# Two weight chunks in a row at one matmul length: regrouped matmuls and four moved or merged steps in a two-block decoder

## The chip, the cores and the metric

One NeuronCore of one Trainium2 chip runs the whole program in one launch. The metric is the device time of an execution in microseconds (us). Two runs are told apart here from about 0.2%, that is 2.5 us.

## The reference

256 tokens of width 1024 pass through two decoder blocks in float32. Cut to what matters:

```
x = x + 0.5*swiglu(rmsnorm(x))                      # ff1, 1024 -> 2816 -> 1024
p = rmsnorm(x) @ w_in                               # gates g_a g_b, u, v, q, k, v of the branches
y_a = u * (W_s @ layernorm(v) + b)                  # spatial gating, branch a
y_b = stick_breaking_attention(q, k, v)             # branch b
x = x + (g_a*(y_a @ w_branch_a) + g_b*(y_b @ w_branch_b)) @ w_out
x = rmsnorm(x + 0.5*swiglu(rmsnorm(x)))             # ff2
h = x + moba(rmsnorm(x)) @ w_o;  h = h + relu(rmsnorm(h) @ w_up)^2 @ w_down      # mlp1
k, v, log_f = (rmsnorm(h)*g_kv) @ (w_kv, w_f)       # log_f: forget gate of 16 heads
h = h + fox(rmsnorm(h) @ w_q, k, v, cumsum(log_f)) @ w_o
h = h + relu(rmsnorm(h) @ w_up)^2 @ w_down                                       # mlp2
return rmsnorm(h)
```

## The kernel before

Nearly all work is weight times activation in float32, done as three products of rounded parts: a weight is split into a high and a low part, an activation too, and high·high, high·low and low·high are summed in PSUM. Weights stream from memory in chunks of 128x1024. For each chunk ScalarE copies the high part (`split_hi`, L140, tile `whi`, 5 buffers), VectorE subtracts it from the raw chunk to get the low part (`split_lo`, L147, tile `wlo`, 4 buffers) and TensorE multiplies (`unit_mm`, L150 to L239, its matmuls at L158).

In a **wide** group the activation's high and low parts lie side by side, so that `whi` takes one matmul of 512 columns where `wlo` takes one of 256. A wide group of the ff1, ff2, gate, gu and mlp stages has 4 chunks of 8 + 8 matmuls and 4 PSUM banks; groups take the banks of two rings (psA, psB) in turn. A down projection (`down`, L593) has 2 groups of 11 or 16 chunks. `orders` sets which kind comes first: high then low in a chunk, low then high in the next.

A unit is one chunk of one group (or a few chunks at the end of a group, `stagger`). The main loop goes over the units and issues, for unit u: the steps registered with `pre`, the high part of chunk u+3 and the low part of chunk u+2, the steps registered with `mid`, the matmuls, and the steps registered with `at`. This fixes the order on every engine; an engine runs its list in that order, and VectorE shares its list between `wlo` subtractions and all evacuations, norms and gating. A `wlo` subtraction needs the `wlo` buffer of four chunks before, so TensorE must be done with that chunk's low matmuls.

A norm (`norm_at`, L407) sums squares on VectorE, reduces them with two matmuls (L440), takes a square root on ScalarE (L443) and a reciprocal on VectorE (L448), while the first group of the stage multiplies the raw activation; the scale is applied to the outputs. The step `f` (L473 to L480) turns the scale into a column with two transposes (L477) and a copy (`rcol`, L479).

Other places that the change touches: `all_gains` (L1333) transposes the norm weights once into `gcol` (L1335 to L1337); `brB` (L906) is the second branch's projection, whose first PSUM banks wait for the gating of the first branch (L920); `fox_f0` to `fox_f4` (L1094 to L1157) compute the forget gate with 24 matmuls (L1104 to L1106) and a scan.

Of the kernel before, what the change touches and what calls it, by code (L numbers as in the profile page):

```python
# [26 lines left out]
class Group:  # L27
# [2 lines left out]

    def __init__(self, ring, srcs, ktiles, xin, tok=False, stagger=0, wide=False):
        self.ring, self.srcs, self.ktiles, self.xin = ring, srcs, ktiles, xin
        self.tok, self.stagger, self.wide = tok, stagger, wide
        self.width = sum(c for _, _, c in srcs)
        self.banks = self.width // (128 if wide else 256)
        self.kph = 1024 // self.width
        self.ps = None
# [3 lines left out]
def decoder_kernel(  # L43
# [58 lines left out]
    def add(g):  # L102
        g.u0 = len(units)
        hs = []
        for k0 in range(0, g.ktiles, g.kph):
            hs.append(len(halves))
            halves.append((g, k0))
        n = len(hs) - g.stagger
        units.extend((g, [h]) for h in hs[:n])
        if g.stagger:  # L110
            units.append((g, hs[n:]))
        g.u1 = len(units) - 1
        return g
# [36 lines left out]
    def unit_mm(u):  # L150
        g, hs = units[u]
        if g.ps is None:
            g.ps = [bank(g.ring) for _ in range(g.banks)]
            g.started = [False] * g.banks
        seq = [(h, kl) for h in hs for kl in range(g.kph)]

        def mm(b, dst, lhsT, rhs, stop):
            PE.matmul(dst, lhsT, rhs, start=not g.started[b], stop=stop, skip_group_check=True)  # L158
            g.started[b] = True

        def orders(i):

            return (("hi", "lo") if i % 2 == 0 or u < 4 else ("lo", "hi")) if g.wide else ((0, 1, 2),)

        def ws(h, kl, b, parts=(0, 1, 2), end=True):
            k = halves[h][1] + kl
            last = end and k == g.ktiles - 1
            if g.wide:
                col = kl * g.width + b * 128
                wh, wl = hi_t[h][:, col:col + 128], lo_t[h][:, col:col + 128]  # L170
                x = g.xin(k, b)
                if parts == "hi":
                    mm(b, g.ps[b], wh, both(x), last)
                elif parts == "lo":
                    mm(b, g.ps[b][:, :T], wl, x[:, 0, :], last)
                for i in parts if len(parts) == 1 else ():
                    mm(b, g.ps[b][:, T:] if i == 1 else g.ps[b][:, :T], wl if i == 2 else wh,
                       x[:, int(i == 1), :], False)
                return
            for j in range(2):  # L180
                nt = 2 * b + j
                col = kl * g.width + nt * 128
                wh, wl = hi_t[h][:, col:col + 128], lo_t[h][:, col:col + 128]
                x = g.xin(k, nt)
                dst = g.ps[b][:, j * T:(j + 1) * T]
                for i in parts:
                    mm(b, dst, wl if i == 2 else wh, x[:, int(i == 1), :], last and j == 1 and i == 2)

        def tsm(h, kl, tok, chs, c=slice(0, 512), d=0):
            k = halves[h][1] + kl  # L190
            last = k == g.ktiles - 1
            nch = g.width // 512
            xh, xl = (g.xin(k, 0)[:, i, tok * 128:(tok + 1) * 128] for i in range(2))
            for w in (hi_t[h], lo_t[h]):
                for ch in chs:
                    col = kl * g.width + ch * 512
                    b = tok * nch + ch + d
                    mm(b, g.ps[b][:, :c.stop - c.start], xh, w[:, col + c.start:col + c.stop], False)
            for ch in chs:
                col = kl * g.width + ch * 512  # L200
                b = tok * nch + ch + d
                mm(b, g.ps[b][:, :c.stop - c.start], xl, hi_t[h][:, col + c.start:col + c.stop], last)

        if g.tok:
            nch = g.width // 512
            if len(hs) > 1:
                for b in range(g.banks):
                    n = 1 if b < g.banks - 1 else 2
                    for i in range(n):
                        if i:  # L210
                            g.ps.append(bank(flip(g.ring)))
                            g.started.append(False)
                        for h, kl in seq:
                            tsm(h, kl, b // nch, (b % nch,), slice(i * 512 // n, (i + 1) * 512 // n), i)
            else:
                for h, kl in seq:
                    for tok in range(2):
                        tsm(h, kl, tok, range(nch))
        elif len(hs) > 1:
            for b in range(g.banks):  # L220
                o = orders(u - g.u0 + b)
                for i in o:
                    for h, kl in seq:
                        ws(h, kl, b, i, i == o[-1])
        elif u == 0:
            for b in range(g.banks):
                if b == 2:
                    x_bank(1)
                for i in range(3):
                    for h, kl in seq:  # L230
                        ws(h, kl, b, (i,))
        else:
            o = orders(u - g.u0)
            for i in o:
                if u == 1 and i == o[-1]:
                    x_turn(3)
                for h, kl in seq:
                    for b in range(g.banks):
                        ws(h, kl, b, i, i == o[-1])  # L239
# [167 lines left out]
    def norm_at(u, ring, two=False, cols=False, own=False):  # L407
# [93 lines left out]
        else:  # L501
            pre(v + 1, d)
        if cols:
            at(u0 + 7, f)

    def colsof(base, i=0):
        return gcol[:, base + 8 * i:base + 8 * i + 8]
# [33 lines left out]
    def ffn(ring, name, wg, wu, wd, slots):  # L541
        r, lead = ring, None
        for i in range(DFF // 256):
            g = add(Group(r, [(wg, 256 * i, 256), (wu, 256 * i, 256)], 8, hn_in, wide=True))
            if lead is None:
                lead = g
                at(g.u0, hidden(name, slots))
                norm_at(g.u0, r, own=True)
# [43 lines left out]

    def down(r, w, ktiles, xin, stagger=2):  # L593

        return [add(Group((r, flip(r))[i], [(w, 512 * i, 512)], ktiles, xin, stagger=i * stagger, wide=True))
                for i in range(2)]

    at(10, w_s_prep, B)
    for i in range(3):
# [33 lines left out]
    gates = []  # L633
    for i in range(4):
        gates.append(add(Group(r, [(win, 5120 + i * 512, 512)], 8, hn_in, wide=True)))
        r = flip(r)
    norm_at(gates[0].u0, gates[0].ring, cols=True, own=True)
    lnp = {}
# [37 lines left out]
    for i in range(2):  # L676
        r = flip(r)
        gu.append(add(Group(r, [(win, 512 * i, 512)], 8, hn_in, wide=True)))

    def gv_evac(b):  # L680
        if b == 0:
# [215 lines left out]
    def last_pv(u, name):  # L897
# [5 lines left out]
    at(qs[0].u1, hidden("yb", (1, 2)))  # L903
    brA = [add(Group(QR, [(w_branch_a[0], 512 * i, 512)], 8, lambda k, nt: xpair(cur["ya"], k)))
           for i in range(2)]
    brB = add(Group(QR, [(w_branch_b[0], 0, D)], 8, fixed_in("yb"), stagger=2))  # L906
    pus = pair_units(qs, vs, 3, 3, 10)
    at(pus[0], S.preload_act_table_set, "natural_log_exp_and_others")
    for p, u in enumerate(pus):
# [129 lines left out]
    def mlp(ring, name, w, slots):  # L1039
        r, lead = ring, None  # L1040
        for i in range(8):
            g = add(Group(r, [(w, 512 * i, 512)], 8, hn_in, wide=True))
            if i == 0:
                at(g.u0, hidden(name, slots))
                norm_at(g.u0, r, own=True)
# [41 lines left out]

    FR = flip(dn[1].ring)
    FP = flip(FR)
    qs, vs = qkv_groups(FR, fox_w_q_2[0], 0, w_kv_2, 0, w_kv_2, D, kv_in, (0, 1), 6, wait=5)  # L1090
    norm_at(qs[0].u0, FP, cols=True)
    fx = {}

    def fox_f0():  # L1094
        fx["wf"] = wf = slot(7, [128, 2, 8, 128], F32R, name="wf")
        nc.gpsimd.memset(raw32(wf), 0.0)
        split(wf[:, 0, :, 0:16], wf[:, 1, :, 0:16], wf_raw)

    def fox_f1():
        wf = fx["wf"]  # L1100
        p = bank(FP)
        for k in range(8):
            h, l = (kv_in(k, 0)[:, i, :] for i in range(2))
            PE.matmul(p[:, :T], wf[:, 0, k, :], h, start=k == 0, stop=False, skip_group_check=True)  # L1104
            PE.matmul(p[:, :T], wf[:, 0, k, :], l, start=False, stop=False, skip_group_check=True)
            PE.matmul(p[:, :T], wf[:, 1, k, :], h, start=False, stop=k == 7, skip_group_check=True)  # L1106
        fx["p"] = p

    def fox_f2():
        fv, av = temp(name="f")[:16, :T], temp(name="fa")[:16, :T]  # L1110
        V.tensor_mul(fv, fx["p"][:16, :T], R["bc"][:16, :])
        V.tensor_scalar(fv, fv, bf_col[:, 0:1], None, op0=OP.add)
        V.tensor_scalar(av, fv, -30.0, None, op0=OP.max)
        S.activation(av, av, AF.Exp, scale=-1.0)
# [33 lines left out]
    u = qs[0].u0  # L1148
    at(u, fox_f0)
    at(u + 2, fox_f1)  # L1150
    pre(u + 5, S.preload_act_table_set, "natural_log_exp_and_others")
    pre(u + 5, fox_f2)
    pre(u + 6, fox_f3)
    at(u + 6, fox_out)
    for j in range(4):
        at(u + 7 + j // 2, fox_f4, j)
    at(u + 9, fox_f3b)  # L1157
    at(u + 11, hidden("ob", (7, 3)))
    wo = add(Group(FR, [(w_o_2[1], 0, D)], 8, fixed_in("ob"), stagger=2))
    soft_attention(qs, vs, FP, "ob", fox_terms, 12, True)  # L1160
# [170 lines left out]
        events.setdefault(i, []).insert(0, (fn, ()))  # L1331

    def all_gains():  # L1333
        p = bank(A)
        PE.transpose(p[:, :128], gains, ident)  # L1335
        V.tensor_copy(gcol[:, 8:128], p[:, 8:128])  # L1336
        V.tensor_mul(gfa, gcol[:, G_FIN:G_FIN + 8], gcol[:, G_AT:G_AT + 8])  # L1337

    at(2, load_consts)
    at(7, all_gains)  # L1340

    for u in range(len(units)):
        for fn, a in before.get(u, []):
# [44 lines left out]
```

## Time and profile before

| what | value |
|---|---|
| median of 3 runs | 1229.07 us (1228.89 to 1229.62) |
| profiled execution | 1229.41 us |
| its span on the core | 1227.6 us |
| TensorE (PE) busy | 1216.4 us, 99%, 7770 matmuls |
| VectorE (DVE) busy | 892.1 us, 73% |
| ScalarE (ACT) busy | 723.7 us, 59% |
| GpSimd (POOL) busy | 2.8 us |
| `wlo` subtractions | 403, 1218 ns each |
| `whi` copies | 403, 1053 ns each |

The span runs from the first to the last recorded work; the profiled execution is 1.8 us longer than it. Busy PE is counted with modelled ends, so its share says that TensorE seldom stands still for long, not that it runs at its peak. In a timeline row, a bracket gives the idle time of the engine ahead of the group and what ended it; shorter waits show only as starts that lie further apart than the work between them.

### The profile page before, as it was taken

How to read it: one execution, taken by the hardware profiler on the slowest of the kernel's cores; microseconds unless marked ns; L12 is line 12 of the kernel's file. 1: busy time of each engine (PE TensorE's matmuls, PEld its weight loads, DVE VectorE, ACT ScalarE, POOL GpSimd, SP SyncE). 2: the span in 40 equal slices, each digit the busy share in tenths (PEclk: the TensorE clock that was granted, in tenths of full speed). 3: DMA queues.
4: the chain of work that ended last, by engine and by line, in shares of the span. 5: the costliest groups of instructions: out<-in, count | busy, mean ns of one | idle time of the engine just before them, and what ended most of it. 6: DMA issues, size and time to landing. Idle time of an engine off the chain costs nothing.

```text
span 1227.6 us, 20221 instructions
## 1 busy us (share of the span) xinstructions
PE 1216.4 (99%) x7770; PEld 1088.1 (89%) x7770; DVE 892.1 (73%) x1451; ACT 723.7 (59%) x1191; POOL 2.8 (0%) x7
## 2 busy tenths in 40 slices
PE   9999999999999999999999999999999999999997
PEld 8888888889999988888899899888889889888886
DVE  7977756769667688778679767977457767887644
ACT  7555545765666567555456756765446566776433
POOL 0000000000000000000000000000000000000000
PEclk9999999999999999999999999999999999999999
DMA  8666656565543565665565445556564634465661
GB/s 273 210 189 190 218 190 190 181 198 155 155 155 124 170 183 178 190 205 175 186 195 159 145 138 172 189 189 208 169 212 133 241 121 154 156 206 189 225 193 46
DMA packets 143409, 219.56 MB, mean 179 GB/s; under 512 B 10088, under 2 KB 81360, under 8 KB 143312
## 3 DMA queue, kind: packets, MB, share of 16 engines
q1 hardware_dynamic: 141568, 213.79, 55.1%
q10 hardware_dynamic: 1744, 4.48, 1.1%
q8 instruction: 61, 1.00, 0.4%
q14 instruction: 36, 0.29, 0.1%
HBM read 217.17 MB, written 1.06 MB: 178 GB/s over the span
## 4 chain that ended last, share of the span: by engine, by line
PE 95%; DVE 4%; issue 0%; ACT 0%; DMA 0%; DVEq 0%; ACTq 0%
PE psA L158 52%; PE psB L158 36%; DVE wlo L147 1%; PE psB L843 1%; PE psB L822 1%; PE psA L843 1%; PE psA L822 1%; PE psB L885 0%; PE psB L728 0%; DMA xin<-in_x_dram 0%; DVE rstd L448 0%; DVE gv L718 0%; PE psB L887 0%; DVE gv L714 0%; DVE st L703 0%
## 5 line engine op out<-in xcount | busy, mean ns | idle before, releaser
L147 DVE TENSOR_TENSOR wlo<-raw,whi 128x1024 fp32r<-128x1024 f32 x403 | 483.6, 1218 | 103.7 <-issue 60.5
L140 ACT ACTIVATE whi<-raw 128x1024 fp32r<-128x1024 f32 x403 | 416.3, 1053 | 136.4 <-PE psA L158 82.1
L158 PE MATMUL psA<-hn,whi 128*128 128x512 f32 (+1 forms) x1224 | 267.6, 345 | 1.0 <-DVE gcol L1336 1.0
L158 PEld LDWEIGHTS psA<-hn,whi 128*128 128x128 f32 x1224 | 209.5, 190 | 26.8 <-DVE gcol L1336 1.5
L158 PE MATMUL psB<-hn,whi 128*128 128x512 f32 (+1 forms) x832 | 197.1, 375 | 0.4 <-DVE rcol L479 0.4
L158 PEld LDWEIGHTS psB<-hn,whi 128*128 128x128 f32 x832 | 149.0, 189 | 25.8 <-DVE rcol L479 0.8
L158 PE MATMUL psA<-hn,wlo 128*128 128x256 f32 x960 | 165.3, 283 | 0.1
L158 PEld LDWEIGHTS psA<-hn,wlo 128*128 128x128 f32 x960 | 139.7, 191 | 4.3 <-DVE wlo L147 0.5
L158 PE MATMUL psB<-hn,wlo 128*128 128x256 f32 x768 | 109.6, 283 | 0.0
L158 PEld LDWEIGHTS psB<-hn,wlo 128*128 128x128 f32 x768 | 102.6, 191 | 3.6
L158 PE MATMUL psA<-whi,mb 128*128 128x512 f32 (+1 forms) x256 | 69.1, 386 | 0.0
L158 PEld LDWEIGHTS psA<-whi,mb 128*128 128x128 f32 x256 | 47.8, 188 | 9.6
L985 ACT ACTIVATE sc<-sc,mx 128x256 f32<-128x256 f32 x64 | 28.4, 445 | 30.7 <-DVE sm L982 30.7
L158 PE MATMUL psA<-whi,hn 128*128 128x512 f32 x128 | 41.7, 395 | 0.0
L158 PE MATMUL psA<-wlo,mb 128*128 128x512 f32 (+1 forms) x128 | 40.3, 386 | 0.0
L158 PE MATMUL psA<-ma,whi 128*128 128x512 f32 x128 | 30.9, 391 | 0.0
L1055 ACT ACTIVATE rl<-rl 128x512 f32<-128x512 f32 x32 | 20.3, 633 | 17.8 <-DVE rl L1052 17.8
L158 PE MATMUL psB<-ma,whi 128*128 128x512 f32 x128 | 30.7, 391 | 0.0
L158 PEld LDWEIGHTS psA<-whi,hn 128*128 128x128 f32 x128 | 24.0, 188 | 5.2
L158 PEld LDWEIGHTS psA<-wlo,mb 128*128 128x128 f32 x128 | 24.0, 188 | 4.9
L383 DVE SCALAR_TENSOR_TENSOR xT<-rs,xT 128x512 f32<-128x512 f32 x16 | 11.0, 688 | 23.7 <-ACT rs L352 23.6
L158 PEld LDWEIGHTS psB<-ma,whi 128*128 128x128 f32 x128 | 23.5, 188 | 4.5
(318 smaller groups left out, 1842.3 us busy)
## 6 DMA issues: line engine op xcount, KB each, us to landing
raw<-in_w_up_dram SPq DMA_DIRECT2D x64, 512.0 KB, 3.8
raw<-in_w_down_dram SPq DMA_DIRECT2D x64, 512.0 KB, 4.4
raw<-in_ff_w_gate_dram SPq DMA_DIRECT2D x88, 256.0 KB, 2.9
raw<-in_ff_w_down_dram SPq DMA_DIRECT2D x44, 512.0 KB, 4.1
raw<-in_ff_w_up_dram SPq DMA_DIRECT2D x86, 256.0 KB, 5.0
raw<-in_w_in_dram SPq DMA_DIRECT2D x40, 512.0 KB, 4.5
raw<-in_w_in_dram SPq DMA_DIRECT2D x32, 256.0 KB, 3.1
raw<-in_moba_w_qkv_dram SPq DMA_DIRECT2D x32, 256.0 KB, 3.5
```

Source lines behind the costliest of these rows:

```text
L140: S.activation(hi_t[h], raw_t[h].rearrange("p k c -> p (k c)"), AF.Copy)
L147: V.tensor_sub(lo_t[h], raw_t.pop(h).rearrange("p k c -> p (k c)"), raw32(hi_t[h]))
L158: PE.matmul(dst, lhsT, rhs, start=not g.started[b], stop=stop, skip_group_check=True)
L383: V.scalar_tensor_tensor(xb, t, alpha, xb, op0=OP.mult, op1=OP.add)
L822: PE.matmul(hb[t][64 * h:64 * h + 64, 384:512], vv[:, k, c:c + 64], w[:, h * 384 + c0:h * 384 + c0 + 128], start=k == 0, stop=k == t, skip ...
L843: PE.matmul(banks[h][:, c:c + n], left[i][rw, cl:cl + 128], right[j][rw, cr:cr + n], start=start and i + j == 0, stop=i == 1, skip_group_c ...
L985: S.activation(s[:, a:b], s[:, a:b], AF.Exp, bias=mx[:, i:i + 1], accum_out=sm[:, i:i + 1])
L1055: S.activation(t, t, AF.Square)
```

## The change

A group can have `pairs` set: all ff groups past the first of their stage, the down projections with more than 8 input tiles, three of the four gate groups, both gu groups and all mlp groups past the first. (The five lines that set it below stand in `ffn`, `down`, the gate loop, the gu loop and `mlp`.) In such a group two chunks a and b go as high(a) high(b) low(b) low(a), and the next two as low low high high. Besides, `all_gains` comes three units later and uses a bank of the other ring; the scale's column of the norm of the gate stage comes one unit earlier; the first two chunks of `brB` become one unit that goes bank by bank (`head=2`); and the forget gate takes 8 matmuls of 512 columns, with the high and low parts of its weights side by side, and comes one unit later, with two more copies and two more additions.

```
+            singles = g.u1 - g.u0 + (len(units[g.u1][1]) == 1)
+            if g.pairs and i < singles - singles % 2:
+                a = u - i % 2
+                hs2 = [units[a][1][0], units[a + 1][1][0]]
+                o = orders(i // 2)
+                for h in hs2 if i % 2 == 0 else hs2[::-1]:
+                    for kl in range(g.kph):
+                        for b in range(g.banks):
+                            ws(h, kl, b, o[i % 2], i % 2 == 1 and h == hs2[1])
+                return
...
-            at(u0 + 7, f)
+            at(u0 + 7 - own, f)
...
+            g.pairs = lead is not None
...
+            g.pairs = ktiles > 8
...
+        gates[-1].pairs = i > 0
...
+        gu[-1].pairs = True
...
+            g.pairs = i > 0
...
-    brB = add(Group(QR, [(w_branch_b[0], 0, D)], 8, fixed_in("yb"), stagger=2))
+    brB = add(Group(QR, [(w_branch_b[0], 0, D)], 8, fixed_in("yb"), stagger=2, head=2))
...
-        fx["wf"] = wf = slot(7, [128, 2, 8, 128], F32R, name="wf")
+        fx["wf"] = wf = slot(7, [128, 8, 128], F32R, name="wf")
...
-            PE.matmul(p[:, :T], wf[:, 0, k, :], h, start=k == 0, stop=False, skip_group_check=True)
-            PE.matmul(p[:, :T], wf[:, 0, k, :], l, start=False, stop=False, skip_group_check=True)
-            PE.matmul(p[:, :T], wf[:, 1, k, :], h, start=False, stop=k == 7, skip_group_check=True)
+            PE.matmul(p, wf[:, k, :], both(kv_in(k, 0)), start=k == 0, stop=k == 7)
+        fx["t"] = t = temp(name="ft")
+        S.activation(t[:16, :T], p[:16, T:], AF.Copy)
+        S.activation(t[:16, T:2 * T], p[32:48, :T], AF.Copy)
...
-        V.tensor_mul(fv, fx["p"][:16, :T], R["bc"][:16, :])
+        V.tensor_add(fv, t[:16, :T], t[:16, T:2 * T])
+        V.tensor_add(fv, fx["p"][:16, :T], fv)
+        V.tensor_mul(fv, fv, R["bc"][:16, :])
...
-    pre(u + 5, fox_f2)
+    pre(u + 6, fox_f2)
...
-        p = bank(A)
+        p = bank(B)
...
-    at(7, all_gains)
+    at(10, all_gains)
```

The order of the instructions shows it at three places. The first is TensorE in the first gu group, one row for each eight matmuls of a part of a chunk (those into the bank psA_2669 with the first of the two input tiles). Before:

```order
L158 MATMUL psA_2669<-hn_1760,whi_2606 128x512
L158 MATMUL psA_2669<-hn_1760,wlo_2626 128x256
L158 MATMUL psA_2669<-hn_1760,wlo_2644 128x256
L158 MATMUL psA_2669<-hn_1760,whi_2624 128x512
L158 MATMUL psA_2669<-hn_1760,whi_2642 128x512
L158 MATMUL psA_2669<-hn_1760,wlo_2664 128x256
L158 MATMUL psA_2669<-hn_1760,wlo_2693 128x256
L158 MATMUL psA_2669<-hn_1760,whi_2662 128x512
```

The same after the change:

```order
L161 MATMUL psA_2669<-hn_1760,whi_2606 128x512
L161 MATMUL psA_2669<-hn_1760,whi_2624 128x512
L161 MATMUL psA_2669<-hn_1760,wlo_2644 128x256
L161 MATMUL psA_2669<-hn_1760,wlo_2626 128x256
L161 MATMUL psA_2669<-hn_1760,wlo_2664 128x256
L161 MATMUL psA_2669<-hn_1760,wlo_2693 128x256
L161 MATMUL psA_2669<-hn_1760,whi_2662 128x512
L161 MATMUL psA_2669<-hn_1760,whi_2642 128x512
```

The low part of the fourth chunk (wlo_2693) moved from seventh to sixth place, ahead of all of the third and fourth chunks' high parts, and the low part of the first chunk (wlo_2626) from second to fourth.

The second is TensorE around the second gate group (psA), where the norm's two matmuls (acc) and the scale's two transposes (ident,rstd) lie between the weights. Before:

```order
L158 MATMUL psA<-hn,whi 128x512 x8
L158 MATMUL psA<-hn,wlo 128x256 x16
L158 MATMUL psA<-hn,whi 128x512 x8
L440 MATMUL psB<-acc,nones 128x256 x2
L158 MATMUL psA<-hn,whi 128x512 x8
L158 MATMUL psA<-hn,wlo 128x256 x16
L158 MATMUL psA<-hn,whi 128x512 x8
L477 MATMUL psB<-ident,rstd 128x128 x2
```

After:

```order
L161 MATMUL psA<-hn,whi 128x512 x16
L161 MATMUL psA<-hn,wlo 128x256 x16
L455 MATMUL psB<-acc,nones 128x256 x2
L161 MATMUL psA<-hn,wlo 128x256 x16
L492 MATMUL psB<-ident,rstd 128x128 x2
L161 MATMUL psA<-hn,whi 128x512 x16
```

The transposes moved from the end of the group to a place with 16 high matmuls behind them, and stand nearer to the norm's matmuls.

The third is VectorE where the forget gate (f, fa, cpad) is made, from the norm's reciprocal on; wlo are weight chunks, qkt the first evacuations of the q and k group. Before:

```order
L448 RECIPROCAL rstd<-rstd 128x256
L470 TENSOR_SCALAR rq<-rstd 128x256
L1111 TENSOR_TENSOR f<-psA,rstd 16x256
L1112 TENSOR_SCALAR f<-f,bf_col 16x256
L1113 TENSOR_SCALAR fa<-f 16x256
L147 TENSOR_TENSOR wlo<-raw,whi 128x1024
L760 TENSOR_TENSOR qkt<-psB,rq 128x512
```

After:

```order
L463 RECIPROCAL rstd<-rstd 128x256
L485 TENSOR_SCALAR rq<-rstd 128x256
L150 TENSOR_TENSOR wlo<-raw,whi 128x1024
L1134 TENSOR_TENSOR f<-ft 16x256
L1135 TENSOR_TENSOR f<-psA,f 16x256
L1136 TENSOR_TENSOR f<-f,rstd 16x256
L1137 TENSOR_SCALAR f<-f,bf_col 16x256
L1138 TENSOR_SCALAR fa<-f 16x256
L150 TENSOR_TENSOR wlo<-raw,whi 128x1024
L781 TENSOR_TENSOR qkt<-psB,rq 128x512
```

One weight chunk's subtraction now stands ahead of the forget gate's first steps, which are five instead of three, and the evacuation of q and k stands behind one more subtraction than before.

## Rows read from the trace of the kernel before

**Rows 1.** The page: span, and shares of the chain of waits by engine.

```profile
span 1227.6 us, 20221 instructions
...
PE 95%; DVE 4%; issue 0%; ACT 0%; DMA 0%; DVEq 0%; ACTq 0%
```

**Rows 2.** Timeline of PE, an ff1 group: start, us, operation, count, [idle before <-releaser].

```profile
78.02 1.98 PE L158 MATMUL psA<-hn,whi 128*128 128x512 f32 x8
79.83 2.08 PE L158 MATMUL psA<-hn,wlo 128*128 128x256 f32 x16
81.74 3.82 PE L158 MATMUL psA<-hn,whi 128*128 128x512 f32 x16
```

**Rows 3.** The chain of waits, mlp1's down projection and the last projection: start, us, what.

```profile
837.00 44.53 PE psB L158 x256
...
1132.40 19.05 PE psA L158 x84
```

**Rows 4.** Timeline of DVE, the same ff1 group: the fourth chunk's low part.

```profile
82.60 1.22 DVE L147 TENSOR_TENSOR wlo<-raw,whi 128x1024 fp32r<-128x1024 f32 x1
```

**Rows 5.** Timeline of PE, the two gu groups.

```profile
262.40 1.98 PE L158 MATMUL psA<-hn,whi 128*128 128x512 f32 x8
...
273.54 1.98 PE L158 MATMUL psB<-hn,whi 128*128 128x512 f32 x8
```

**Rows 6.** Timeline of DVE, low parts of the second gu group's first and fourth chunks.

```profile
265.43 1.23 DVE L147 TENSOR_TENSOR wlo<-raw,whi 128x1024 fp32r<-128x1024 f32 x1 [1.51 <-PE psA L158]
...
280.61 1.22 DVE L147 TENSOR_TENSOR wlo<-raw,whi 128x1024 fp32r<-128x1024 f32 x1
```

**Rows 7.** Timeline of PE, third groups of ff1, ff2 and mlp1.

```profile
31.63 0.94 PE L158 MATMUL psA<-hn,whi 128*128 128x512 f32 x3
33.61 1.43 PE L158 MATMUL psA<-hn,whi 128*128 128x512 f32 x5 [1.04 <-DVE gcol L1336]
...
473.08 1.98 PE L158 MATMUL psB<-hn,whi 128*128 128x512 f32 x8
...
769.91 1.98 PE L158 MATMUL psB<-hn,whi 128*128 128x512 f32 x8
...
777.29 2.20 PE L158 MATMUL psB<-hn,wlo 128*128 128x256 f32 x16
```

**Rows 8.** Timeline of DVE, the same groups: gcol copy, low parts of fourth chunks.

```profile
33.28 0.28 DVE L1336 COPY gcol<-psA 128x120 f32<-128x120 f32 x1
...
38.92 1.22 DVE L147 TENSOR_TENSOR wlo<-raw,whi 128x1024 fp32r<-128x1024 f32 x1
...
479.50 1.22 DVE L147 TENSOR_TENSOR wlo<-raw,whi 128x1024 fp32r<-128x1024 f32 x1
...
777.00 1.22 DVE L147 TENSOR_TENSOR wlo<-raw,whi 128x1024 fp32r<-128x1024 f32 x1
```

**Rows 9.** Timeline of PE, start of the third gate group.

```profile
217.63 0.94 PE L158 MATMUL psB<-hn,whi 128*128 128x512 f32 x3
218.94 1.43 PE L158 MATMUL psB<-hn,whi 128*128 128x512 f32 x5 [0.36 <-DVE rcol L479]
```

**Rows 10.** Timeline of DVE, the gate stage: the norm's reciprocal.

```profile
212.60 1.75 DVE L448 RECIPROCAL rstd<-rstd 128x256 f32<-128x256 f32 x1 [3.81 <-ACT rstd L443]
```

**Rows 11.** Timeline of PE, brB's first banks, and first v chunk of the fox stage.

```profile
403.47 0.47 PE L158 MATMUL psA<-yb,whi 128*128 128x256 f32 x2 [0.26 <-DVE gate L920]
...
952.19 0.48 PE L158 MATMUL psB<-whi,kv 128*128 128x512 f32 x1
953.37 0.50 PE L158 MATMUL psB<-wlo,kv 128*128 128x512 f32 x1 [0.70 <-DVE wlo L147]
```

**Rows 12.** Timeline of DVE, the fox stage: low part of the third v chunk.

```profile
956.96 1.22 DVE L147 TENSOR_TENSOR wlo<-raw,whi 128x1024 fp32r<-128x1024 f32 x1
```

**Rows 13.** Windows after the last matmul: length, PE busy, granted clock, DMA share, GB/s.

```profile
1221.40:1225.60 4.20, 0.00 (x0) 1.00 0.25 98
1225.70:1227.60 1.90, 0.00 (x0) 0.50 0.12 43
```

More of the change, by code (lines that the diff above doesn't have):

```diff
@@ L27, with __init__ @@
 class Group:
-    def __init__(self, ring, srcs, ktiles, xin, tok=False, stagger=0, wide=False):
+    def __init__(self, ring, srcs, ktiles, xin, tok=False, stagger=0, wide=False, head=0):
+        self.head, self.pairs = head, False
         self.ring, self.srcs, self.ktiles, self.xin = ring, srcs, ktiles, xin
@@ L108, in add @@
         n = len(hs) - g.stagger
-        units.extend((g, [h]) for h in hs[:n])
+        if g.head:
+            units.append((g, hs[:g.head]))
+        units.extend((g, [h]) for h in hs[g.head:n])
         if g.stagger:
@@ L232, in unit_mm @@
         else:
-            o = orders(u - g.u0)
+            i = u - g.u0
+            singles = g.u1 - g.u0 + (len(units[g.u1][1]) == 1)
[8 more added lines that the diff above has]
+                return
+            o = orders(i)
             for i in o:
@@ L593, in down @@
     def down(r, w, ktiles, xin, stagger=2):
-        return [add(Group((r, flip(r))[i], [(w, 512 * i, 512)], ktiles, xin, stagger=i * stagger, wide=True))
-                for i in range(2)]
+        gs = [add(Group((r, flip(r))[i], [(w, 512 * i, 512)], ktiles, xin, stagger=i * stagger, wide=True))
+              for i in range(2)]
+        for g in gs:
+            g.pairs = ktiles > 8
+        return gs
     at(10, w_s_prep, B)
@@ L1089, in decoder_kernel @@
     FP = flip(FR)
-    qs, vs = qkv_groups(FR, fox_w_q_2[0], 0, w_kv_2, 0, w_kv_2, D, kv_in, (0, 1), 6, wait=5)
+    qs, vs = qkv_groups(FR, fox_w_q_2[0], 0, w_kv_2, 0, w_kv_2, D, kv_in, (0, 1), 6, wait=6)
     norm_at(qs[0].u0, FP, cols=True)
@@ L1094, in fox_f0 @@
     def fox_f0():
-        fx["wf"] = wf = slot(7, [128, 2, 8, 128], F32R, name="wf")
+        fx["wf"] = wf = slot(7, [128, 8, 128], F32R, name="wf")
         nc.gpsimd.memset(raw32(wf), 0.0)
-        split(wf[:, 0, :, 0:16], wf[:, 1, :, 0:16], wf_raw)
+        split(wf[:, :, 0:16], wf[:, :, 32:48], wf_raw)
     def fox_f1():
@@ L1102, in fox_f1 @@
         for k in range(8):
-            h, l = (kv_in(k, 0)[:, i, :] for i in range(2))
-            PE.matmul(p[:, :T], wf[:, 0, k, :], h, start=k == 0, stop=False, skip_group_check=True)
-            PE.matmul(p[:, :T], wf[:, 0, k, :], l, start=False, stop=False, skip_group_check=True)
-            PE.matmul(p[:, :T], wf[:, 1, k, :], h, start=False, stop=k == 7, skip_group_check=True)
+            PE.matmul(p, wf[:, k, :], both(kv_in(k, 0)), start=k == 0, stop=k == 7)
+        fx["t"] = t = temp(name="ft")
+        S.activation(t[:16, :T], p[:16, T:], AF.Copy)
+        S.activation(t[:16, T:2 * T], p[32:48, :T], AF.Copy)
         fx["p"] = p
@@ L1110, in fox_f2 @@
         fv, av = temp(name="f")[:16, :T], temp(name="fa")[:16, :T]
-        V.tensor_mul(fv, fx["p"][:16, :T], R["bc"][:16, :])
+        t = fx["t"]
+        V.tensor_add(fv, t[:16, :T], t[:16, T:2 * T])
+        V.tensor_add(fv, fx["p"][:16, :T], fv)
+        V.tensor_mul(fv, fv, R["bc"][:16, :])
         V.tensor_scalar(fv, fv, bf_col[:, 0:1], None, op0=OP.add)
@@ L1150, in decoder_kernel @@
     at(u + 2, fox_f1)
-    pre(u + 5, S.preload_act_table_set, "natural_log_exp_and_others")
-    pre(u + 5, fox_f2)
-    pre(u + 6, fox_f3)
-    at(u + 6, fox_out)
+    pre(u + 6, S.preload_act_table_set, "natural_log_exp_and_others")
+    pre(u + 6, fox_f2)
+    pre(u + 7, fox_f3)
+    at(u + 7, fox_out)
     for j in range(4):
-        at(u + 7 + j // 2, fox_f4, j)
-    at(u + 9, fox_f3b)
+        at(u + 8 + j // 2, fox_f4, j)
+    at(u + 10, fox_f3b)
     at(u + 11, hidden("ob", (7, 3)))
```

## The prediction

> **What bounds the kernel now.** I read the page first. The span is 1227.6 us, and the chain of waits is PE for 95% and DVE for 4% [rows 1]. TensorE's own stream sets the time nearly everywhere, so time can be won by fewer or shorter matmuls, or at the few places where PE waits. A measurement of this kernel can tell a difference of over 0.2%, 2.46 us, from no change.
>
> Next comes PE's timeline in a steady group [rows 2]: eight high matmuls last 1.81 us (78.02 to 79.83), sixteen low ones 1.91 (79.83 to 81.74). The chain has 84 matmuls of 512 columns in 19.05 us, 0.2268 each [rows 3]; a low one takes 0.12. A group without a wait is 32 × 0.3468 = 11.10 us.
>
> Then DVE's timeline, since the waits of PE end on DVE. What counts is the offset in its group at which PE wants a low part. Before, the fourth chunk's low part stands behind 24 high and 24 low matmuls, 24 × 0.2268 + 24 × 0.12 = 8.32 us. After, it stands behind 16 high and 24 low ones, 6.51 us: it is **due 1.81 us sooner**. The third chunk's is due as much sooner (7.36 to 5.55). The first chunk's low part, which was done with at 2.77, is done with at 5.55, so **its buffer comes free 2.78 us later**. DVE's own list hardly changes, so each place where DVE is now early by less than these amounts must be looked up.
>
> **The change part by part.**
>
> *Regrouping, what it wins.* A run of 256 alternating matmuls took 44.53 us [rows 3], and 128 × 0.3468 is 44.39. The rest, 0.14, lies at 8 returns from low to high, 0.0175 each. Thirty-nine paired groups lose one return of two, the down projections 21 more: 60 × 0.0175 = **−1.05 us**. The Trainium skill, "TensorE: Matmul & The Clock Gate", section "Back-to-back issue gap", gives a matmul's gap as its columns over 2.4 GHz plus 2.5 ns, whatever stood ahead of it; by it this term would be 0 and the sum 1 us higher. The row is longer than its matmuls alone, so I keep the term.
>
> *Regrouping, where it binds not.* In a steady ff group that starts at 78.02 [rows 2] the fourth low part is ready at 82.60 + 1.22 = 83.82 [rows 4] and due, after the change, at 78.02 + 6.51 = 84.53. It has 0.7 us left, so most groups stay free of waits.
>
> *Regrouping, third groups of a stage.* There DVE is catching up after the norm's reciprocal, for which all evacuations of the first group waited, and works without a pause: its rows there [rows 8] have no bracket for idle time.
> - mlp1: start 769.91, due 776.42 [rows 7], ready 777.00 + 1.22 + 0.06 for the signal = 778.28 [rows 8]. PE waits 1.86 us. The 0.12 that it waits there already goes (sixteen low matmuls take 2.20 there and 2.08 in the steady group) [rows 2, 7].
> - mlp2 has the same list in the same place: the same again. Both together **+3.72 and −0.24**.
> - ff2: start 473.08 [rows 7], due 479.59, ready 479.50 + 1.22 = 480.72 [rows 8]: **+1.15**.
> - ff1: before, PE stood here for gcol: three high matmuls lasted from 31.63 to 33.61, 1.98 us instead of 0.68 [rows 7]. The norm weights now come later and to the other ring, so this wait goes: **−1.30**. But the group now reaches its fourth low part at 31.63 + 6.51 = 38.14, and that is ready at 38.92 + 1.22 = 40.14, less some 0.4 because gcol's copy (0.28, and a small product behind it) has left DVE's list [rows 8]: 39.75, **+1.6**. The saved wait is taken back.
>
> *Regrouping, the gu groups.* The low part of the second group's first chunk runs at 265.43, and DVE had waited 1.51 us for PE to give the buffer free [rows 6]. PE gives it after 262.40 + 5.55 = 267.95 [rows 5] now, 2.75 us later than before. All that DVE has behind it, the layer norm of v and three more low parts, is one list without slack. The fourth low part, ready at 280.61 + 1.22 = 281.83 before [rows 6], comes at 284.6. It is due at 273.54 + 6.51 = 280.05 [rows 5]. PE waits **+4.6** in two pieces: the third chunk's low part, one place ahead in DVE's list, is late by 0.9, and so the second piece is 3.7 us long. This is the dearest place.
>
> *The scale's column, one unit earlier.* The wait on rcol before the third gate group goes: three high matmuls took 1.31 us instead of 0.68 [rows 9], **−0.63**. In exchange PE comes to the transposes before 16 high matmuls, at about 217.63 − 0.1 (the two transposes) − 3.63 = 213.9, while the reciprocal ends at 212.60 + 1.75 = 214.35 [rows 10]. With the signals on the way PE waits about 0.6: **+0.6**.
>
> *brB.* Bank by bank, the second bank is reached later than its gating: **−0.26** [rows 11].
>
> *Forget gate.* 24 × 0.12 = 2.88 us become 8 × 0.2268 = 1.81: **−1.06**. The two more additions and copies on 16 rows have no row; the nearest is the 0.28 of gcol's copy [rows 8], the upper end a subtraction's 1.22 [rows 8] each. I take 0.3 to 0.4. They are hidden on ScalarE, and on DVE count in the next lines. The wait at the first v chunk goes, since its low part moves ahead of the gate: 952.19 to 953.37 is 1.18 us instead of 0.23, **−0.95** [rows 11]. PE then reaches v at 951.13. A v chunk is 12 matmuls of 512 columns, 2.72 us, and so the third chunk's low part is due at 951.13 + 5.44 + 0.23 = 956.8. DVE's list up to it has the same reciprocal ahead and ends at 956.96 + 1.13 = 958.1 [rows 12], give or take the additions: about **+1.1**. The biases of the fox attention are loaded one unit later; the queues' order is otherwise the same, and I cost that at nothing because the attention starts only after all v chunks. Were this cover gone it would cost up to the unit, about 2.7 us.
>
> *Small waits.* Idle figures count from modelled ends (0.70 where the starts give 0.95) [rows 11], so brB's is short by about as much, and PE's small waits on low parts after the gu groups go too: I put **−0.8** for them, an estimate.
>
> *Sum.* Wins 1.05 + 0.24 + 1.30 + 0.63 + 0.26 + 1.06 + 0.95 + 0.8 = 6.3. Losses 3.72 + 1.15 + 1.6 + 4.6 + 0.6 + 1.1 = 12.8. Together **+6.5 us**. The profiled execution took 1229.41 us: the span of 1227.6 and 1.8 around it. It becomes 1235.9; the median of the runs was 0.34 below it, so I say **1235.6 us**.
>
> **The rivals.**
>
> *It is faster: the new due times do not bind.* If DVE gets each low part done before 6.51 us into its group, all losses of the third groups and of gu are gone and the wins stay: only the 0.6 and 1.1 that do not come from the regrouping remain: 1229.1 − 6.3 + 1.7 = 1224.5. For it: the slack in steady groups, and that DVE is idle a good part of the time. Against it: at the five places DVE's rows touch one another. The point that decides is whether the subtraction behind the reciprocal ends before PE comes. Chance 0.08.
>
> *About the same: half of it binds.* If DVE's list starts 1 us sooner at the third groups, because something ahead of the reciprocal ends sooner, and gu's wait is half, the losses shrink by 4 + 2.3, and it comes out at 1235.6 − 6.3 = 1229.3. Chance 0.09.
>
> *Slower, but less: the buffer does not hold DVE in gu.* If the first chunk's buffer came free in time, the fourth low part stays at 281.83 and the wait is 281.83 − 280.05 = 1.8 instead of 4.6: 1232.8. Against it stands the bracket of 1.51 us on PE [rows 6]. Chance 0.10.
>
> *Slower still: the clock falls in gu's wait.* After the last matmul the granted clock stayed at 1.00 for a stretch of 4.2 us without matmuls and was 0.50 in the next [rows 13]. That speaks against it: the wait in gu is 3.7 us. For it speaks that the two are close. At 1.2 instead of 2.4 GHz the 8 low and 16 high matmuls behind it would take 4.6 us more; half of that, as the clock may rise in between, gives 1237.9, all of it 1240.2. The Trainium skill, "TensorE: Matmul & The Clock Gate", section "Why this matters for your kernels", says that gaps between bursts of matmuls bring the clock back to half; no run here shows it inside this kernel. Chance 0.13.
>
> That the change does not do what it says is left out: the order shows every piece of it.
>
> **How the numbers follow.** Forecast 0.60, faster 0.08, half 0.09, gu less 0.10, clock 0.13. The forecast's own range is 1233.5 to 1238, from 1.2 either way for the third groups' start and for gu. With gu's case and half of the clock's it is 1231 to 1239; the half case adds its upper part down to 1230.5. Left out are the faster case, part of the half case and the upper half of the clock's. Faster by over 0.2% (under 1226.6) is the first rival: 0.08. Within 0.2% is the half case: 0.09. Slower is the rest: 0.83.
>
> **What would show it.** In the profile after: a PE row of low matmuls released by DVE wlo in the third group of ff1, ff2, mlp1 and mlp2, with 1 to 2 us each; the low part of the second gu group's first chunk on DVE waiting 4.2 us on PE instead of 1.51, and PE idle 3 to 4 us there; no wait on gcol, rcol before the third gate group, or the first v chunk; 8 forget matmuls in 1.81 us; a down group of 256 matmuls in some 44.45. The forecast is wrong if those waits on wlo are missing, or if further groups, the steady ones, wait too, for there are 39 of them and 0.3 us in each would be 12 us.

## The result and the profile after

The changed kernel took 1237.44 us (median of 6 runs, 1236.22 to 1239.37) against 1229.30 us before (6 runs, 1228.83 to 1229.65): 1.0068 times as long, 95% interval 1.0058 to 1.0078. It is slower by 8.1 us where 6.5 were forecast, inside the stated range. The six runs lie in two groups, three at 1236.2 to 1236.6 us with a mean granted clock of 0.998 to 0.999 and three at 1238.3 to 1239.4 with 0.995 to 0.996; the profiled execution, 1239.37 us with a span of 1237.6, is of the second.

The page of the changed kernel, answering to [rows 1]:

```profile
span 1237.6 us, 20196 instructions
...
PE 91%; DVE 6%; DMA 1%; issue 1%; ACT 1%; DVEq 0%; ACTq 0%; SPq 0%
```

DVE's share of the chain rose from 4% to 6%. The view of waits says what PE waits for (total, times, longest, in us):

```profile
PE psB L161 <- DVE wlo L150: 7.2, 5, 3.4
PE psA L161 <- DVE wlo L150: 2.8, 2, 1.7
...
PE psB L492 <- DVE rstd L463: 0.4, 1, 0.4
```

Before, PE waited once for a low part, 0.70 us [rows 11]. Now it waits seven times, 10.0 us together, the longest 3.4. Five of the seven are shown below; the other two are 0.27 us in ff1's second group and 0.71 us in the fox stage. The waits on gcol, rcol and the gate of brB [rows 7, 9, 11] are no longer there.

PE's timeline in the two gu groups, answering to [rows 5]:

```profile
262.05 3.79 PE L161 MATMUL psA<-hn,whi 128*128 128x512 f32 x16
265.68 4.00 PE L161 MATMUL psA<-hn,wlo 128*128 128x256 f32 x32
269.51 3.82 PE L161 MATMUL psA<-hn,whi 128*128 128x512 f32 x16
273.16 3.79 PE L161 MATMUL psB<-hn,whi 128*128 128x512 f32 x16
276.79 3.15 PE L161 MATMUL psB<-hn,wlo 128*128 128x256 f32 x24
283.34 2.08 PE L161 MATMUL psB<-hn,wlo 128*128 128x256 f32 x8 [3.41 <-DVE wlo L150]
285.22 5.74 PE L161 MATMUL psB<-hn,whi 128*128 128x512 f32 x16
290.80 0.40 PE L161 MATMUL psA<-hn,whi 128*128 128x256 f32 x2
```

PE stands 3.41 us for the fourth low part. Behind that wait two things are odd: the 8 low matmuls last 1.88 us (283.34 to 285.22) and the 16 high ones 5.58 (285.22 to 290.80), where behind the wait in mlp1, shown further down, they last 1.06 and 3.66. The windows of PE there show why (length, PE busy, granted clock, DMA share, GB/s):

```profile
273.20:279.80 6.60, 6.60 (x41) 1.00 0.27 80
279.90:283.30 3.40, 0.03 (x1) 0.88 0.47 149
283.40:288.80 5.40, 5.40 (x17) 0.50 0.50 150
288.90:295.00 6.10, 6.10 (x44) 0.97 0.48 134
```

The clock was at 1.00 while PE worked, fell during the wait, stayed at 0.50, the lower level, for 5.4 us of unbroken work and then rose. That costs 0.82 + 1.92 = 2.7 us on top of the wait. DVE's timeline, answering to [rows 6]:

```profile
262.33 1.23 DVE L150 TENSOR_TENSOR wlo<-raw,whi 128x1024 fp32r<-128x1024 f32 x1 [1.97 <-ACT whi L143]
266.88 1.22 DVE L150 TENSOR_TENSOR wlo<-raw,whi 128x1024 fp32r<-128x1024 f32 x1 [3.33 <-PE psA L161]
...
282.07 1.22 DVE L150 TENSOR_TENSOR wlo<-raw,whi 128x1024 fp32r<-128x1024 f32 x1
```

DVE waits 3.33 us on PE for the buffer instead of 1.51, and the fourth low part is ready at 283.29 instead of 281.83. The group starts 0.35 us earlier than before; counted from that start, DVE begins the low part at 4.83 us (266.88 − 262.05) instead of 3.03 (265.43 − 262.40), and the fourth low part is ready 1.8 us later too.

PE in the third groups of ff1, ff2, mlp1 and mlp2, answering to [rows 7] (one row per wait, and in the last three the 16 high matmuls behind it):

```profile
39.34 1.22 PE L161 MATMUL psA<-hn,wlo 128*128 128x256 f32 x8 [1.07 <-DVE wlo L150]
...
485.66 1.21 PE L161 MATMUL psB<-hn,wlo 128*128 128x256 f32 x8 [1.06 <-DVE wlo L150]
486.71 3.82 PE L161 MATMUL psB<-hn,whi 128*128 128x512 f32 x16
...
784.14 1.22 PE L161 MATMUL psB<-hn,wlo 128*128 128x256 f32 x8 [1.72 <-DVE wlo L150]
785.20 3.82 PE L161 MATMUL psB<-hn,whi 128*128 128x512 f32 x16
...
1080.35 1.40 PE L161 MATMUL psA<-hn,wlo 128*128 128x256 f32 x8 [1.72 <-DVE wlo L150]
1081.55 5.25 PE L161 MATMUL psA<-hn,whi 128*128 128x512 f32 x16
```

All four wait, as forecast, though ff1 less long than its 1.6. The two MLPs wait equally long, but behind mlp2's wait the 16 high matmuls take 5.25 us instead of 3.82. The windows around both, first two rows of mlp1, then three of mlp2, show the clock there too:

```profile
782.50:784.10 1.60, 0.00 (x0) 1.00 0.62 232
784.20:788.80 4.60, 4.60 (x24) 1.00 0.64 199
...
1078.70:1080.30 1.60, 0.00 (x0) 1.00 0.66 246
1080.40:1083.20 2.80, 2.80 (x12) 0.64 0.57 176
1083.30:1086.60 3.30, 3.30 (x13) 0.80 0.90 266
```

The chain gives the steady groups and mlp1's down projection, answering to [rows 3]:

```profile
55.87 11.11 PE psA L161 x64
...
844.58 44.45 PE psB L161 x256
```

Taken between the starts of the same groups in the two timelines, the 10.0 us between the spans fall out as follows:

| stretch | before | after | change | forecast |
|---|---|---|---|---|
| start, to ff1's second group | 20.17 | 19.72 | −0.45 | 0 |
| ff1, second and third group | 24.45 | 24.87 | +0.42 | +0.3 |
| gate stage | 45.71 | 45.63 | −0.08 | −0.03 |
| gu groups | 22.37 | 28.75 | +6.38 | +4.6 |
| behind gu, to the end of brB | 143.5 | 142.4 | −1.1 | −1.06 |
| ff2, third group | 11.13 | 12.42 | +1.29 | +1.15 |
| mlp1, third group | 11.26 | 13.09 | +1.83 | +1.74 |
| fox stage | 116.8 | 116.1 | −0.7 | −0.9 |
| mlp2, third group | 11.25 | 14.66 | +3.41 | +1.74 |
| all other groups | | | −1.0 | −1.05 |

The start is the landing of the first input, which differs from run to run; the last line is not measured group by group but is what remains of the 10.0. The +6.38 in gu is a wait of 3.7 by the starts (the 24 low matmuls ahead of it take 24 × 0.12 = 2.9 of the 6.55 from 276.79 to 283.34) and the 2.7 of the clock; of mlp2's +3.41 some 1.6 is the clock.

### The profile page after: what moved, and what is told of

It is laid out like the page before. It is cut to its first block, busy times and chain, and to the rows that moved or that the text cites. A ratio compares the mean times of both kernels' runs of the same rounds, so it can differ in the third digit from the quotient of the medians.

```text
span 1237.6 us, 20196 instructions
## 1 busy us (share of the span) xinstructions
PE 1219.1 (99%) x7754; PEld 1090.3 (88%) x7754; DVE 893.7 (72%) x1453; ACT 724.2 (59%) x1193; POOL 1.9 (0%) x7
## 3 DMA queue, kind: packets, MB, share of 16 engines
HBM read 217.17 MB, written 1.06 MB: 176 GB/s over the span
## 4 chain that ended last, share of the span: by engine, by line
PE 91%; DVE 6%; DMA 1%; issue 1%; ACT 1%; DVEq 0%; ACTq 0%; SPq 0%
PE psA L161 50%; PE psB L161 35%; DVE wlo L150 2%; PE psB L864 1%; PE psB L843 1%; DVE rstd L463 1%; PE psA L864 1%; PE psA L843 1%; PE psB L906 0%; DVE rl L1074 0%; DVE rl L373 0%; DMA raw<-in_ff_w_gate_dram 0%; PE psB L749 0%; DMA xin<-in_x_dram 0%; PE psB L908 0%
## 5 line engine op out<-in xcount | busy, mean ns | idle before, releaser
L161 PE MATMUL psA<-hn,whi 128*128 128x512 f32 (+1 forms) x1224 | 264.4, 346 | 0.0
L161 PEld LDWEIGHTS psA<-hn,whi 128*128 128x128 f32 x1224 | 212.2, 190 | 27.3 <-DVE hn L1323 0.4
L161 PE MATMUL psB<-hn,whi 128*128 128x512 f32 (+1 forms) x832 | 194.6, 377 | 0.0
L161 PEld LDWEIGHTS psB<-hn,whi 128*128 128x128 f32 x832 | 152.0, 190 | 26.8
L161 PEld LDWEIGHTS psA<-ma,whi 128*128 128x128 f32 x128 | 23.6, 188 | 4.6
```

## The experiments

The theory: the regrouping makes the third and fourth low part of a group due 1.8 us sooner, and PE waits wherever DVE's list is not that far ahead; in gu a late buffer adds to it; and the wait there lets the clock fall. The rivals: another edit loses the time, the regrouping loses by something in the pairs themselves, or PE is slow in gu for a reason of its own. Each experiment is named by what it does; diffs are against the changed kernel unless said otherwise.

**The change without its regrouping**

```
-            if g.pairs and i < singles - singles % 2:
+            if False and g.pairs and i < singles - singles % 2:
```

> The change without its regrouping: the norm weights, the scale's column, brB and the forget gate stay as changed. Theory (the regrouping alone loses the time, the other edits win): the wait on gcol (1.3 us), the wait on rcol (0.6), brB's wait (0.5) and some 0.7 in the fox stage are gone against the kernel before: about 1226.0 us. Rival (one of the other edits loses by itself, the forget gate's longer list on DVE first of all): 1228 to 1230 us.

Measured: 1226.14 us (8 runs, 1225.93 to 1227.29), 0.9973 times the kernel before (0.9963 to 0.9984). The small edits win 3.2 us, so the regrouping loses some 11 in the changed kernel. The rival is out.

**The regrouping alone** (the regrouping's lines put into the kernel before, nothing else)

```
+            g.pairs = lead is not None
...
+            if g.pairs and i < singles - singles % 2:
...
```

> The regrouping alone, put into the kernel before. Theory: 1.0 us won by fewer returns from low to high parts, lost 0.7 in ff1 (the wait on gcol stays, so less is waited there), 1.3 in ff2, 1.8 in each MLP, 3.3 in the gu groups, and up to 3 and 1.5 us more where the clock falls behind the waits of gu and of an MLP: 1236.5 to 1240 us. Rival (the regrouping loses only together with the moved steps): within 2.5 us of 1229.3.

Measured: 1238.80 us (4 runs, 1238.52 to 1240.18), 1.0077 times before (1.0062 to 1.0092). It loses alone. Its wait in gu is the same 3.41 us, and again the matmuls behind it are slow: 2.08 for 8 low and 5.42 for 16 high ones.

**The gu groups in the old order**

```
-        gu[-1].pairs = True
```

> The changed kernel with the two gu groups in the old order. Theory (the wait of 3.4 us in the second gu group makes the clock fall there): the gu groups take 22.4 us as in the kernel before instead of 28.7, the clock stays at 1.00 in them; 1231.5 to 1232.5 us, and 1.5 more in a run where the clock falls in an MLP. Rival (the fall of the clock has another cause, and comes by itself in this part of the program): the clock is 0.50 there again and the time 1234 to 1236 us.

Measured: 1233.16 us (9 runs, 1231.70 to 1234.17). The gu stage is as before, with no wait and the clock at 1.00, and the rival is out, though the median lies 0.7 above the 1231.5 to 1232.5 of the forecast. The two gu groups alone cost the changed kernel 4.3 us of median. The profiled run, 1232.79 us, shows the waits of 1.7 us in both MLPs with the clock up in both; runs reach 2.5 us higher than the lowest. A clock that falls behind one of these waits in some runs would do that, but it was not seen.

**Five buffers for low parts**

```
-LO = 4
+LO = 5
...
-            split_lo(units[u][1][-1] + LO - 2)
+            split_lo(units[u][1][-1] + 2)
```

> The changed kernel with five buffers for low parts instead of four, the subtractions in the same order. Theory (in gu DVE waits for a buffer, and its list behind it comes late by that): DVE's wait of 3.3 us on PE before the low part of the second gu group's first chunk is gone, PE's wait of 3.4 us in that group is under 1.8, the clock stays up there; the waits in the third groups of ff1, ff2 and the MLPs stay at 1.1 to 1.7 us, for there DVE is busy without a pause: about 1232 us. Rival (DVE is simply too busy in gu): the wait there stays over 3 us and the time at 1236 to 1238 us.

Measured: 1234.77 us (5 runs, 1233.28 to 1235.19), 1.0039 times before. The mechanism is as expected, the time 2.8 us above the forecast, and the fastest run still 1.3. In the profiled run, at 1233.28 the fastest, the wait on the buffer is gone from DVE's timeline, the same low part now waits for its high part on ACT, and PE's wait in gu is 1.08 us with the 16 high matmuls behind it at their usual length. DVE's timeline:

```profile
265.03 1.23 DVE L150 TENSOR_TENSOR wlo<-raw,whi 128x1024 fp32r<-128x1024 f32 x1 [0.87 <-ACT whi L143]
```

and PE's, behind it:

```profile
281.50 1.22 PE L161 MATMUL psB<-hn,wlo 128*128 128x256 f32 x8 [1.08 <-DVE wlo L150]
282.56 3.82 PE L161 MATMUL psB<-hn,whi 128*128 128x512 f32 x16
```

The waits in the third groups stay at up to 1.7 us. Three of the five runs have a mean clock of 0.997 instead of 0.998 to 0.999 and take some 1.5 us more; where it fell in them stays open.

**Zeros multiplied during the wait**

```
...
+                    if g is WARM[0] and i == 2 and h == hs2[1]:
+                        x = g.xin(0, 0)
+                        for j in range(12):
+                            mm(j % 4, g.ps[j % 4], zer, both(x), False)
...
```

> The changed kernel with 12 matmuls of 512 columns by a block of zeros (2.7 us, they add nothing to the sums) put ahead of the late low part in the second gu group, where PE stands for 3.4 us. Theory (the wait lets the clock fall, and the fall is a cost of its own): the low part starts when it did, 3.5 to 3.6 us behind the third one's end, but 8 low and 16 high matmuls behind it take 4.7 us instead of 7.5, the clock stays at 1.00 there: about 1236 us at most in all runs, or 1234.5 to 1236. Rival (PE is slow there because of something other than its idle time, such as DMA traffic): still 7 us or more for them, and the time rises by what the added matmuls take.

(The lines left out make the block `zer` and set `WARM[0]` to the second gu group.)

Measured: 1235.43 us (4 runs, 1235.04 to 1236.31), so 2.0 us of median less than the changed kernel with 12 matmuls more. All four runs have a mean clock of 0.998 to 0.999, as only three of the changed kernel's six have; those three are 0.8 to 1.1 us above this median, the other three 2.9 to 3.9. PE's timeline in gu:

```profile
277.00 3.15 PE L162 MATMUL psB<-hn,wlo 128*128 128x256 f32 x24
279.99 2.91 PE L162 MATMUL psB<-hn,zer 128*128 128x512 f32 x12
283.56 1.22 PE L162 MATMUL psB<-hn,wlo 128*128 128x256 f32 x8 [0.66 <-DVE wlo L151]
284.62 3.82 PE L162 MATMUL psB<-hn,whi 128*128 128x512 f32 x16
288.27 0.40 PE L162 MATMUL psA<-hn,whi 128*128 128x256 f32 x2
```

The late low part starts 6.56 us after the 24 low ones ahead of it began (277.00 to 283.56), as in the changed kernel (276.79 to 283.34, 6.55), so the wait itself is the same. The matmuls behind it take 4.71 us (283.56 to 288.27) instead of 7.46 (283.34 to 290.80). The windows during the zeros and behind the wait both have the clock at 1.00:

```profile
280.20:282.90 2.70, 2.70 (x12) 1.00 0.56 184
...
284.00:287.60 3.60, 3.60 (x21) 1.00 0.45 146
```

So the fall of the clock is a cost of its own, 2.75 us by this comparison of two profiled executions, and it goes when PE is kept at work through the same wait, with a DMA share of 0.56 and 0.45 in these windows against 0.47 and 0.50 in the changed kernel. The rival falls.

**The old order in gu and in the second and third groups**

```
-            g.pairs = lead is not None
+            g.pairs = i > 2
...
-        gu[-1].pairs = True
...
-            g.pairs = i > 0
+            g.pairs = i > 2
```

(the first in `ffn`, the last in `mlp`)

> The changed kernel with the old order in the gu groups and in the second and third groups of ff1, ff2 and both MLPs. Theory (the regrouping costs only where DVE comes late, and wins 0.02 us in every other group): no wait on a low part over 0.6 us, the clock at 1.00 throughout, and against the change without regrouping (1226.1) 0.9 us won in steady groups and down projections and 0.5 lost at the gate groups' transposes: 1225.7 us, runs within 1 us of each other. Rival (the regrouped steady groups wait too or draw the clock down): 1227 us or more.

Measured: 1226.11 us (8 runs, 1225.56 to 1227.30), 0.9975 times before (0.9965 to 0.9985). The view of PE's waits has one wait on a low part left, the one in the fox stage:

```profile
PE psB L161 <- DVE wlo L150: 0.7, 1, 0.7
PE psB L492 <- DVE rstd L463: 0.4, 1, 0.4
```

The steady groups neither wait nor lower the clock. This places the loss in the groups put back, which are the five places named ahead and the second groups beside them; the only wait there in the changed kernel is the 0.27 us in ff1. The time is that of the change without its regrouping (1226.14), so the 0.4 us that the remaining regrouping was to win does not show in the runs.

**The same, and the gate groups in the old order**

```
-        gates[-1].pairs = i > 0
```

> As the kernel before it in this call, and the gate groups in the old order too. Theory: the wait of 0.44 us of the two transposes on the reciprocal goes and three times 0.02 us is given up: 1225.2 us. Rival (the place of the transposes does not matter on the path): the same time as the one before.

Measured: 1225.51 us (6 runs, 1224.91 to 1226.28), 0.9969 times before (0.9958 to 0.9981). The wait of the transposes on the reciprocal is gone from the view of waits, and the median is 0.6 lower, though the two ranges overlap. This version is faster than both kernels: 3.9 us less than the one before, 11.9 less than the changed one. Against the change without its regrouping it is 0.6 lower, less than the runs can tell apart, so nearly all of the 3.9 comes from the small edits.

**Every pair as high high low low**

```
-                o = orders(i // 2)
+                o = ("hi", "lo")
```

> The changed kernel with every pair as high high low low, so that the second pair no longer begins with its low parts: the fourth low part is due 9.2 to 10.1 us into its group instead of 6.5, the low matmuls of a group again have two returns to high ones, and the first chunk's buffer comes free as late as in the changed kernel. Theory (what costs is the earlier due time, not taking two chunks in a row): no wait on a low part over 0.7 us in the third groups and in gu, the clock stays up; about the time of the change without regrouping, 1226 to 1227 us. Rival (pairs cost by themselves, through buffers freed later): waits of 1 us and more stay in gu at least, 1229 us or more.

Measured: 1227.33 us (11 runs, 1226.87 to 1228.15), 0.9984 times before (0.9975 to 0.9993). Every group that was paired is still paired, and the loss is gone. In gu DVE waits for the buffer as long as in the changed kernel, 3.33 us, but PE only 0.81. DVE's timeline:

```profile
265.79 1.23 DVE L150 TENSOR_TENSOR wlo<-raw,whi 128x1024 fp32r<-128x1024 f32 x1 [3.33 <-PE psA L161]
```

and PE's timeline of the same kernel:

```profile
282.25 2.17 PE L161 MATMUL psB<-hn,wlo 128*128 128x256 f32 x16 [0.81 <-DVE wlo L150]
```

That 0.81 and a wait of 0.83 just behind gu are over the limit of 0.7 that was expected; they may be the 0.3 us by which the time is above the forecast. So the due time is what costs, not the pairing.

**Low(a) ahead of low(b) in the first pair**

```
-                for h in hs2 if i % 2 == 0 else hs2[::-1]:
+                for h in hs2 if i < 2 else hs2[::-1] if i % 2 else hs2:
```

> The changed kernel with low(a) ahead of low(b) in a group's first pair. It asks which buffer the low part of the second gu group's first chunk waits for. If it is the one that is given free first, whichever chunk held it, DVE starts it 0.25 us behind the group's first eight low matmuls as before, 4.8 us into the first gu group, and the time stays at 1236 to 1239.5 us. If it is the second chunk's by name, DVE starts it 0.96 us later than in the changed kernel, 5.8 us into that group, and PE's wait in gu grows from 3.4 to 4.4 us.

One run: 1238.51 us. DVE starts that low part at 267.09, 4.84 us into the first gu group (262.25), as in the changed kernel (4.83), though the first eight low matmuls now belong to the other chunk. A buffer is reused in the order in which it comes free, whichever chunk held it. DVE's timeline:

```profile
267.09 1.23 DVE L150 TENSOR_TENSOR wlo<-raw,whi 128x1024 fp32r<-128x1024 f32 x1 [3.33 <-PE psA L161]
```

and PE's, at the first gu group's start and around the wait:

```profile
262.25 3.79 PE L161 MATMUL psA<-hn,whi 128*128 128x512 f32 x16
...
283.56 1.22 PE L161 MATMUL psB<-hn,wlo 128*128 128x256 f32 x8 [3.42 <-DVE wlo L150]
284.62 5.42 PE L161 MATMUL psB<-hn,whi 128*128 128x512 f32 x16
289.87 0.40 PE L161 MATMUL psA<-hn,whi 128*128 128x256 f32 x2
```

The wait is the changed kernel's, but the 24 matmuls behind it take 6.31 us (283.56 to 289.87), not 7.46: the same wait costs a different amount of clock in another execution.

**The old forget gate** (against the change without its regrouping: the 24 matmuls, their events and the wait put back)

```
-            PE.matmul(p, wf[:, k, :], both(kv_in(k, 0)), start=k == 0, stop=k == 7)
+            PE.matmul(p[:, :T], wf[:, 0, k, :], h, start=k == 0, stop=False, skip_group_check=True)
+            PE.matmul(p[:, :T], wf[:, 0, k, :], l, start=False, stop=False, skip_group_check=True)
+            PE.matmul(p[:, :T], wf[:, 1, k, :], h, start=False, stop=k == 7, skip_group_check=True)
...
```

> The change without its regrouping and with the old forget gate, so that norm weights, the scale's column and brB alone are left. Theory (the forget gate's 1.06 us are half given back, since DVE's longer list makes the third v chunk's low part late by 0.95): 1226.6 us, 0.4 over the run with the new forget gate. Rival (the new forget gate wins its full 1.06 and the old wait's 0.95): 1228 us.

Measured: 1226.82 us (11 runs, 1226.20 to 1227.67), 0.7 above the run with the new forget gate, nearer to the theory's 0.4 than to the rival's 2, though a difference this small is not clear of noise. PE's timeline of that run has the old wait at the first v chunk; the run with the new gate has two others, at the second and third chunk, and eight matmuls of 1.84 us in place of 2.88:

```profile
950.79 0.50 PE L161 MATMUL psB<-wlo,kv 128*128 128x512 f32 x1 [0.70 <-DVE wlo L150]
```

```profile
931.67 2.00 PE L1125 MATMUL psA<-kv,wf 128*128 128x512 f32 x8
...
951.74 0.50 PE L161 MATMUL psB<-wlo,kv 128*128 128x512 f32 x1 [0.23 <-DVE wlo L150]
955.47 0.50 PE L161 MATMUL psB<-wlo,kv 128*128 128x512 f32 x1 [0.71 <-DVE wlo L150]
```

By the timelines the matmuls are 1.04 us shorter, and DVE's longer list only moves the wait.

## Why the prediction was right, and where it was off

The sign and the mechanism of the waits hold: 1237.44 against 1235.6, from waits that stand where the prediction put them. That the size comes so near is in part luck: a wait in gu put too long by some 0.9 us and a clock put at nothing, which cost 2.7 + 1.6 us in the profiled execution, pull in opposite ways. Point by point:

- *What the regrouping wins.* 11.13 became 11.11 us per group and 44.53 became 44.45 in the down projection: 0.02 and 0.08 against the forecast's 0.0175 and 0.07. About 1.0 us, as forecast. The formula of the Trainium skill, "TensorE: Matmul & The Clock Gate", section "Back-to-back issue gap", which that page gives for an isolated matmul and which has no term for what stood ahead, would have made it nothing; the measured groups decide for the row.
- *Third groups.* ff1, ff2 and mlp1 came out within 0.15 us of the working, ff1 only by its net: its wait is 1.07 us, not 1.6, and 0.27 in its second group was not forecast. DVE's list in mlp1 is not quite without a pause, as the working has it: before, it waits 0.23 us on ACT once ahead of that low part. That high high low low takes the waits away shows the due time as the cause; that five buffers leave them shows that buffers are not.
- *The gu groups.* The fourth low part came 3.6 us late (283.29, due at 273.16 + 6.51 = 279.67), not 4.6, and in one piece; PE does not wait for the third. The step that failed is "PE gives it after 262.40 + 5.55 = 267.95": it took DVE to wait for the first chunk's buffer, as the description of the kernel ahead of it does ("the `wlo` buffer of four chunks before"). DVE goes on at the first buffer that PE gives free, after the first eight low matmuls, 4.6 us into the group. It came 1.8 us later into the group than before, not 2.75; the 0.95 between them is eight low matmuls.
- *The clock.* The rival of 0.13 came true beside the forecast, in some of the runs. The prediction let it speak against the rival that the wait in gu, 3.7 us, is shorter than the 4.2 us without matmuls through which the clock stayed up after the last matmul [rows 13]. The clock fell all the same in the profiled run, at a cost of 2.7 us in gu and 1.6 in mlp2. The zeros show cause and price. It did not fall so in every run: 5.4 us at half the clock lower the mean over the span by 0.002, and the run of 1236.22 us has a mean of 0.999, that of the kernel before. That run, 0.6 us above the forecast, had the forecast's own case. The row in the Trainium skill, "TensorE: Matmul & The Clock Gate", section "Why this matters for your kernels", on gaps that bring the clock back to half is borne out by the window of gu at 0.50; mlp1's wait shows that not every gap does it.
- *Moved steps.* The waits on gcol, rcol and brB's gate went as forecast. The transposes in the gate stage wait 0.44 us on the reciprocal, 0.60 by the starts (211.59 + 16 × 0.12 = 213.51, and they start at 214.11), as forecast. The version without it has the lowest median.
- *Fox.* 24 matmuls of 2.88 us became 8 of 1.84, and the wait moved to a later chunk; −0.7 net against −0.9. The working's own figures make the new wait 958.1 − 956.8 = 1.3, where the sum has 1.1; with 1.3 the net is −0.7.

What stays open: why equal waits of 1.72 us let the clock fall in mlp2 and not in mlp1 of the same execution, why the 3.4 us in gu cost less clock in one execution than in another, and where it fell in the runs without a profile.

## What to carry to other kernels

An order that uses an operand sooner is to be checked against the engine that makes the operand, group by group: here the regrouped groups together win about 1 us by their rows, and the five places where VectorE was late lost some 14 in the profiled execution, 4.3 of it through the clock. Read the new due time of each operand off the matmuls ahead of it and compare it with the end of the row that makes it; regroup only where that leaves room. Here that turned 8 us of loss into 4 of gain, but 3.2 of the 4 come with no regrouping at all, and the rest is too small for the runs to tell. A wait of TensorE can cost more than its length, through the clock of the matmuls behind it: 2.7 us behind the 3.4 in gu.

## What the runs showed of the hardware that was not expected

- The granted clock fell to 0.50 in a PE wait of 3.4 us in the middle of the kernel, and stayed there for 5.4 us of unbroken matmuls; 24 matmuls took 7.46 us instead of 4.71. Behind the same wait in the run with low(a) ahead of low(b) they took 6.31. After the last matmul it had stayed at 1.00 through 4.2 us without matmuls [rows 13].
- Two waits of 1.72 us in one execution: behind one the clock stayed at 1.00, behind the other it fell to 0.64 on average over 2.8 us. In the profiled executions of five other kernels with both waits it fell behind mlp2's once more (low(a) ahead of low(b), 6.27 us for the 24 matmuls instead of 4.72) and behind mlp1's never.
- Matmuls by a block of zeros, put into a wait, kept the clock up in the profiled run and won 2.0 us of median.
